# RWKV-7 inside a hybrid decoder layer: the substitution as a step of its own, the fourth unit prepared ahead of the third's solve

## The chip, the cores and the metric

One core of one Trainium2 chip. The metric is the device time of one execution in microseconds (us). A kernel's time is the median of several runs.

## What is computed

One layer of a decoder trunk on 1024 tokens of width 1024, in float32. One projection of the normalised input feeds three mixers side by side: a convolution group (256 columns), sparse attention (512 columns: 8 query heads with a compressed, a selected and a window branch) and RWKV-7 (256 columns: 4 heads of 64). Their outputs are put side by side, go through one output projection and are added to the residual; a gated feed-forward part follows. The change touches the RWKV part, which is, per head and token (cut from the reference, in its words shortened):

```
state = state * decay + (state @ -kk) outer (kk * a) + v outer k
y     = state @ r
y     = group_norm(y) * gain + bias
out   = (y + bonus * v) * gate
```

The recurrence is run in chunks of 32 tokens. Inside a chunk the terms that tie one token to the next form a triangular system; its inverse is built by substitution, row after row.

## The kernel before

Every product is float32 in three terms of high and low parts (`mm3`, L235, on TensorE; `split` makes the parts, L120 on ScalarE and L121 on VectorE). RWKV's work is cut into four units (j, h): j is a pair of heads, h a half of the tokens (512). Each unit passes three steps:

- start: `rwkv_prep` (decays, keys; L405 on) and `rwkv_mats` (L506 to L561). `rwkv_mats` makes the chunk matrices (L524 masks them, L538), stores the triangular ones to memory (`dn`, L529), makes `VA` and `KB` (L543, L544), loads all chunks' triangles into `sN` (L532) and runs the substitution on GpSimd, 31 pairs of a product and a sum (L554, L556), and stores the inverse (L560, L561).
- solve (`rwkv_solve`): loads the inverse into the tile that the triangles were in (`TT` is another view of `sN`) and applies it (L582, L589, L601 on TensorE).
- chain (`rwkv_chain`): the recurrence over 16 chunks (L617, L618, L623, L630, L634, L637), group norm (L643 to L654: mean, square on ScalarE, variance, an inverse root by Newton steps in `rsqrt`, L106 to L116), transposes (L657), gain and bias (`gz`, L659), bonus (L660), the gate product (L662, L663), and the store into `md` (L664).

`md` is a scratch tensor in memory that holds the three mixers' outputs. The steps are traced in the order of a string in L25; units (0, 0) and (0, 1) are traced ahead of attention's preparation, units (1, 0) and (1, 1) at the end of it. All steps of the units are traced with a high priority, and a scheduler then fixes every engine's order of instructions from its own model of when things are ready; on the chip each engine and SyncE's (SP) DMA queue keep that order.

Attention runs by query tiles in the order 7, 6, 5, 4, 0, 3, 2, 1 (`attn_tile`): compressed scores (L865 on TensorE, L870 and L873 on VectorE, L875 on GpSimd, L876 on ScalarE, L878 on VectorE, L883 on GpSimd, L888 and L891 on TensorE), then for four heads each a window and a selected branch (L919 and L920 scores, L923 mask and maximum from PSUM, L930 exponential, L932, L937 scaling of the probabilities, L944 transposes, L947, L952 product with the values). L958 takes a tile's result, L959 stores it to `md`. Beside it GpSimd makes sums of the feed-forward's down weights (`down_sums`, L971 to L974; loads L969, stores L977). They are tied to the substitutions: `issue_after(us[1, int(n > 1)].sub)`.

The output projection (`mix_load`, L1010; `out_tile`, L235, L1027) begins with tile 7 of the tokens, so with `md` columns that unit (1, 1) writes. Its weights are loaded at L994 and split in advance.

Of the kernel before, what the change touches and what calls it, by code (L numbers as in the profile page):

```python
# [19 lines left out]
class K:  # L20
    def __init__(self, tc, a, out, ctx, bufs=None):
        self.tc, self.nc, self.a, self.out, self.ctx = tc, tc.nc, a, out, ctx
        self.B = dict(b2=20, wraw=2, whi=2, wlo=2, t4=4, rraw=2, cy=2, hx=12, ev=3, cv=2, lora=2, rb=20, at=2, pr=7, rt=2,
                      QS=2, pp=6, q8=2, pT=5, pace=31, xn=8, ds=((), (0, 1, 2), (3, 4), (5, 6, 7), (8, 9), (10,), (), ()), h2=14, graw=2, prod=5, ft=4, u=4, wr2=4, wfh=3, wfl=3, S=2, p1=2, om=6, grow=2, pre=2, ap=(), wf=("own", "wf", "om"), hd=("vector",) * 4, tq=((0, 1, 2, 3),), ttag=("tr", "rw"),
                      mm=3, tr=2, av=1, rw=2, mm1=2, tr1=2, pm=2, early="00 01", ga=2, gb=1, gc=1, y=16, r4=15, ta=3, tb=4, mid=2, de=dict(S3="gpsimd", T3="vector", T1="gpsimd", T2="gpsimd", T4="vector", S1="gpsimd", S2="gpsimd", S4="gpsimd"), order=(7, 6, 5, 4, 0, 3, 2, 1), sc=0, pk=1280, st="sync", last=5, sub="gpsimd",  steps="lora r0 S00 conv taps pa V00 S01 pb keys q C00 V01 C01 r1a cmp0 cend r1b cmp1 r1c S10 V10 S11 C10 V11 C11", both=0, cm="gpsimd", rpu=(), wo="vector", tap=(0, 31), vt="cv", vs="vector", va={1: (0, 1), 3: (2, 3), 5: (4, 5), 7: (6, 7)}, vq="sync", vl=1, vw=1, t1=("pm", "tr1"), into={6: (6, 2), 4: (4, 2), 3: (3, 1), 2: (2, 1), 1: (1, 1), 0: (0, 1)})  # L25
        self.B.update(bufs or {})
        P_ = lambda n, **k: ctx.enter_context(tc.tile_pool(name=n, **k))
        self.cst = P_("cst", bufs=1)
        self.sm = P_("sm", bufs=4)
        self.big = P_("big", bufs=1)  # L30
        self.mcp = tc.tile_pool(name="mc", bufs=1)
        self.mc = self.mcp.__enter__()
        self.dram = P_("dram", bufs=1, space=bass.MemoryType.DRAM)
        self.uid = 0
        self.st = getattr(tc.nc, self.B["st"])
        self.xp = self.psp = None
# [470 lines left out]
    def rwkv_mats(self, u):  # L507
        nc = self.nc
        v, s, pe = nc.vector, nc.scalar, nc.tensor
        dn = self.dram.tile([32, 32, 32], F32, name=f"dn{u.j}{u.h}")  # L510
        u.dt = self.dram.tile([16, 32, 4, 8], F32, name=f"dt{u.j}{u.h}")
        u.dtt = self.dram.tile([32, 8, 4, 32], F32, name=f"dtt{u.j}{u.h}")

        u.GA, u.GR = ([self.rb([P, 8, 64], name=n) for _ in range(2)] for n in ("GA", "GR"))
        for q in range(2):
            pts = [self.bank(u.tp) for _ in range(2)]
            for c in range(4):
                for hp in range(2):
                    r = slice(hp * 64, hp * 64 + 64)
                    pe.matmul(pts[hp][:, c * P:c * P + P], u.BK[q][r, c].rearrange("p a t -> p (a t)"),  # L520
                              u.AR[q][r, c].rearrange("p a t -> p (a t)"), start=True, stop=True)
            for x, G in enumerate((u.GA, u.GR)):
                for hp in range(2):
                    v.tensor_tensor(G[hp][:, q * 4:q * 4 + 4, :], pts[hp].rearrange("p (a b) -> p a b", b=P)[:, :, x * 64:x * 64 + 64],  # L524
                                    self.gmask[:, x * 64:x * 64 + 64].unsqueeze(1).to_broadcast([P, 4, 64]), op=ALU.mult)
        for hp in range(2):
            for blk in range(2):
                p0 = blk * 16 + hp * 8
                nc.sync.dma_start(dn[p0:p0 + 8].rearrange("p s t -> s p t"), u.GA[hp][64 + blk * 32:96 + blk * 32, :, blk * 32:blk * 32 + 32])  # L529
        N = self.sN.rearrange("p (a b) -> p a b", b=32)  # L530
        for g in range(4):
            nc.sync.dma_start(N[g * 32:g * 32 + 32], dn)  # L532
        u.VA, u.KB = [], []
        for q in range(2):
            VA = self.rb([P, 4, P], name="VA")
            KB = self.rb([P, 4, P], name="KB")
            BK = u.BK[q].rearrange("p c a t -> p c (a t)")
            v.tensor_tensor(BK, BK, u.PC[:, q * 4:q * 4 + 4].unsqueeze(2).to_broadcast([P, 4, P]), op=ALU.mult)  # L538
            for dst in (VA, KB):
                pt = self.bank(u.tp)  # L540
                for c in range(4):
                    x = u.VAc[q][:, c].rearrange("p a t -> p (a t)") if dst is VA else BK[:, c, :]
                    pe.transpose(pt[:, c * P:c * P + P], x, self.idn)  # L543
                s.activation(dst.rearrange("p c x -> p (c x)"), pt, AF.Copy)  # L544
            u.VA.append(VA)
            u.KB.append(KB)

        Tm = self.sT
        nc.gpsimd.tensor_copy(Tm, self.sI)
        for q in range(31):  # L550
            n, w = 31 - q, q // 4 + 1
            x = self.sx[:, 0:n * w].rearrange("p (a b) -> p a b", b=w)
            v_ = getattr(nc, self.B["sub"])
            v_.tensor_tensor(x, N[:, q, q + 1:32].unsqueeze(2).to_broadcast([P, n, w]),  # L554
                            Tm[:, q, 0:w].unsqueeze(1).to_broadcast([P, n, w]), op=ALU.mult)
            u.sub = v_.tensor_tensor(Tm[:, q + 1:32, 0:w], Tm[:, q + 1:32, 0:w], x, op=ALU.add).ins  # L556
        sTT = self.sTT.rearrange("p a b -> p (a b)").rearrange("p (a b) -> p a b", b=32)
        v.tensor_copy(sTT, Tm.rearrange("p a b -> p b a"))
        for g in range(4):
            nc.sync.dma_start(u.dt[:, :, g, :], Tm[g * 32:g * 32 + 16])  # L560
            nc.sync.dma_start(u.dtt[:, :, g, :], sTT[g * 32:g * 32 + 32])  # L561
# [740 lines left out]
    def build(self):  # L1302
        order = self.B["order"]
        self.fill = []
        nc, a = self.nc, self.a
# [29 lines left out]
        us = {}  # L1335

        def start(j, h):
            with self.tc.high_priority(offset=100000):
                us[j, h] = self.rwkv_prep(j, h)
                self.rwkv_mats(us[j, h])  # L1340

        def solve(j, h):
            with self.tc.high_priority(offset=100000):
                self.rwkv_solve(us[j, h])

        def chain(j, h):
            with self.tc.high_priority(offset=100000):
                self.rwkv_chain(us[j, h])
        steps = dict(lora=lambda: self.rwkv_lora(hT), keys=lambda: self.attn_keys(hT), q=lambda: self.attn_q(hT),
                     cmp=lambda: self.attn_cmp(hT), conv=lambda: self.conv_proj(hT), taps=self.conv_taps, pa=lambda: self.conv_pool(range(20), us[0, 0].sub), pb=lambda: self.conv_pool(range(20, 31), us[0, 1].sub), cend=self.conv_rest, r0=lambda: self.rwkv_proj(0, hT),  # L1350
                     r1=lambda: self.rwkv_proj(1, hT), cmp0=lambda: self.attn_cmp(hT, (0,)), cmp1=lambda: self.attn_cmp(hT, (1,)),
                     r1a=lambda: self.rwkv_proj(1, hT, (0,)), r1b=lambda: self.rwkv_proj(1, hT, (1,)), r1c=lambda: self.rwkv_proj(1, hT, (2,)))
        for st in self.B["steps"].split():
            if st[0] in "SVC" and len(st) == 3:
                dict(S=start, V=solve, C=chain)[st[0]](int(st[1]), int(st[2]))
            else:
                steps[st]()
        self.phase("2")
# [86 lines left out]
```

## Time and profile before

| | us |
|---|---|
| median of 3 runs | 1489.62 (1488.12 to 1493.52) |
| the profiled execution | 1485.23 |
| its span, first to last instruction | 1483.7 |
| PE busy | 1396.1 (94%) |
| DVE busy | 1014.7 (68%) |
| ACT busy | 686.1 (46%) |
| POOL busy | 501.2 (34%) |

PE is TensorE's matmuls, PEld its weight loads, DVE VectorE, ACT ScalarE, POOL GpSimd, SP SyncE, whose instructions here are DMA issues. A matmul's end is modelled, so a busy PE is not PE at its peak. PEclk is TensorE's granted clock as a share of full speed. All times count from the span's start; attention lies between about 381 and 701 us. "idle before <-releaser" is the time in which the engine stood ahead of an instruction, and what ended it.

### The profile page before, as it was taken

What the parts mean: (1) busy time and instruction counts of PE and PEld (TensorE: products, weight loads), DVE (VectorE), ACT (ScalarE), POOL (GpSimd) and SP (SyncE); (2) the same over time, 40 slices, a digit from 0 to 9 for tenths busy, and PEclk for the clock granted to TensorE, in tenths of its full rate; (3) what the DMA queues carried; (4) which work ended last, traced back from release to release, by engine and by line L of the source; (5) the groups of instructions that cost most, each with busy time, mean ns of one, the idle gap of its engine ahead of it and who ended that gap; (6) DMA issues with size and microseconds to landing.
All of it is one profiled execution on the core that took longest, in us unless ns stands there. A gap on an engine that the chain in (4) does not pass through costs nothing.

```text
span 1483.7 us, 22736 instructions
## 1 busy us (share of the span) xinstructions
PE 1396.1 (94%) x7897; PEld 1100.5 (74%) x7897; DVE 1014.7 (68%) x2187; ACT 686.1 (46%) x1377; POOL 501.2 (34%) x607
## 2 busy tenths in 40 slices
PE   6999888899899999898799899999999999999997
PEld 5887666677677777576578677788788788888886
DVE  6343799355777788988357767676775776656685
ACT  5432454353466766677233443344333334445463
POOL 1001898830106407540000143443444452113310
PEclk9999898999899999999899899999999999999999
DMA  6133324525412612863641123332332334986523
GB/s 184 40 106 82 68 78 125 142 76 171 114 44 55 189 48 59 259 221 100 202 160 52 41 86 97 107 103 71 107 114 93 107 100 158 386 285 213 186 92 114
DMA packets 206678, 186.68 MB, mean 126 GB/s; under 512 B 56355, under 2 KB 145764, under 8 KB 206564
## 3 DMA queue, kind: packets, MB, share of 16 engines
q1 hardware_dynamic: 206564, 185.24, 40.2%
q8 instruction: 62, 1.02, 0.3%
q14 instruction: 52, 0.43, 0.1%
HBM read 126.99 MB, written 58.20 MB: 125 GB/s over the span
## 4 chain that ended last, share of the span: by engine, by line
PE 76%; DVE 11%; POOL 4%; issue 3%; DMA 3%; ACT 1%; SPq 1%; DVEq 0%; ACTq 0%; POOLq 0%
PE gb L235 13%; PE mm L235 10%; PE rw L235 10%; PE ga L235 9%; PE gc L235 8%; PE tr L235 5%; PE tr L944 4%; PE av L952 4%; PE mm L919 2%; POOL sT L556 2%; POOL sx L554 2%; PE mm L920 2%; DVE cacc L277 1%; DVE pp L923 1%; DVE pp L937 1%
## 5 line engine op out<-in xcount | busy, mean ns | idle before, releaser
L235 PE MATMUL mm<-hT,whi 128*128 128x512 f32 x608 | 198.4, 408 | 5.9 <-ACT whi L120 4.3
L235 PEld LDWEIGHTS mm<-hT,whi 128*128 128x128 f32 x608 | 116.2, 194 | 35.6 <-ACT whi L120 5.0
L235 PE MATMUL mm<-hT,wlo 128*128 128x512 f32 x304 | 123.6, 409 | 3.1 <-DVE wlo L121 2.9
L947 ACT ACTIVATE pT<-tr 128x512 f32<-128x512 f32 (+1 forms) x152 | 79.5, 534 | 46.6 <-PE tr L944 45.5
L294 POOL TENSOR_TENSOR cacc<-cacc,ctap 128x512 f32<-128x512 f32 x60 | 98.1, 1661 | 5.4 <-ACT ctap L292 4.7
L952 PE MATMUL av<-pT,V 128*64 128x128 f32 x1056 | 93.3, 287 | 1.6 <-ACT pT L947 1.6
L944 PE MATMUL tr<-idn,pp 128*128 128x128 f32 x528 | 90.7, 289 | 0.4 <-DVE pp L937 0.3
L121 DVE TENSOR_TENSOR sp<-rb,sp 128x512 fp32r<-128x512 f32 x66 | 56.6, 858 | 49.1 <-ACT sp L120 49.0
L235 PE MATMUL rw<-woh,mix 128*128 128x512 f32 x240 | 77.9, 400 | 9.5 <-ACT mix L120 6.6
L235 PE MATMUL rw<-sp,sp 128*128 128x512 f32 x330 | 86.2, 389 | 0.0
L235 PE MATMUL tr<-sp,sp 128*128 128x512 f32 x330 | 85.9, 389 | 0.0
L919 PE MATMUL mm<-KH,QS 128*128 128x512 f32 (+2 forms) x192 | 76.5, 403 | 9.2 <-DVE mx L923 8.0
L952 PEld LDWEIGHTS av<-pT,V 128*64 128x64 f32 x1056 | 56.9, 136 | 30.1 <-issue 15.8
L944 PEld LDWEIGHTS tr<-idn,pp 128*128 128x128 f32 x528 | 56.2, 141 | 30.3 <-issue 28.4
L120 ACT ACTIVATE sp<-rb 128x512 fp32r<-128x512 f32 x66 | 41.6, 630 | 74.4 <-PE tr L235 39.1
L121 DVE TENSOR_TENSOR sp<-b,sp 128x512 fp32r<-128x512 f32 x88 | 70.8, 814 | 4.9 <-ACT sp L120 4.8
L937 DVE TENSOR_SCALAR pp<-pp,sm 128x640 f32<-128x640 f32 (+7 forms) x128 | 72.9, 610 | 1.1
L235 PEld LDWEIGHTS mm<-hT,wlo 128*128 128x128 f32 x304 | 58.6, 193 | 18.5 <-DVE wlo L121 4.7
L1106 POOL TENSOR_TENSOR S<-wraw,wr 128x512 f32<-128x512 f32 x22 | 28.5, 1296 | 127.8 <-DVE wlo L121 46.7
L235 PEld LDWEIGHTS rw<-sp,sp 128*128 128x128 f32 x330 | 61.9, 188 | 13.1 <-ACT sp L120 0.3
L235 PEld LDWEIGHTS tr<-sp,sp 128*128 128x128 f32 x330 | 61.9, 188 | 12.9
L121 DVE TENSOR_TENSOR wlo<-wraw,whi 128x512 fp32r<-128x512 f32 x55 | 45.9, 837 | 35.2 <-ACT whi L120 32.9
(455 smaller groups left out, 3658.4 us busy)
## 6 DMA issues: line engine op xcount, KB each, us to landing
wraw<-in_ffn_w_up_dram SPq DMA_DIRECT2D x44, 256.0 KB
wr<-in_ffn_w_gate_dram SPq DMA_DIRECT2D x44, 256.0 KB
pdS<-prod SPq DMA_DIRECT2D x44, 256.0 KB
b<-pdS SPq DMA_DIRECT2D x44, 256.0 KB
rb<-tdT SPq DMA_DIRECT2D x44, 256.0 KB
pdA<-prod SPq DMA_DIRECT2D x33, 256.0 KB
b<-pdA SPq DMA_DIRECT2D x33, 256.0 KB
wraw<-in_w_in_dram SPq DMA_DIRECT2D x30, 256.0 KB
```

Of the source, the lines that this page charges most:

```text
L120: self.nc.scalar.activation(hi, src, AF.Copy)
L121: return getattr(self.nc, eng).tensor_tensor(lo, src, hi.bitcast(F32), op=ALU.subtract).ins
L235: mm = lambda l, r, **k: self.nc.tensor.matmul(out, l, r, skip_group_check=more, **k)
L294: nc.gpsimd.tensor_tensor(t[:, o:o + 512], t[:, o:o + 512], z, op=ALU.add)
L554: v_.tensor_tensor(x, N[:, q, q + 1:32].unsqueeze(2).to_broadcast([P, n, w]), Tm[:, q, 0:w].unsqueeze(1).to_broadcast([P, n, w]), op=ALU.mult)
L556: u.sub = v_.tensor_tensor(Tm[:, q + 1:32, 0:w], Tm[:, q + 1:32, 0:w], x, op=ALU.add).ins
L919: pe.matmul(pts[g][:, 0:n], QS[:, r, g, :], KH[g][hf][:, ks], start=True, stop=False)
L920: pe.matmul(pts[g][:, 0:n], QS[:, r, g, :], KL[g][hf][:, ks], start=False, stop=True)
L937: v.tensor_scalar(Ps[g], Ps[g], sm[:, g:g + 1], None, op0=ALU.mult)
L944: pe.transpose(pt[:, o:o + P], Ps[g][:, kt * P:kt * P + P], self.idn)
L947: s.activation(pT[:, 0:n], pt[:, 0:n], AF.Copy)
L952: pe.matmul(av[g * 64:g * 64 + 64, r * P:r * P + P], self.V[kk // 2][:, kk % 2, vo + g * 64:vo + g * 64 + 64], pT[:, o:o + P], start=first ...
```

## The change

`rwkv_mats` ends with `VA` and `KB`. What stood in it for the substitution, from the loads of `sN` to the stores of the inverse, becomes `rwkv_sub`, a step "B" of its own. In the string of steps B follows S at once for units (0, 0), (0, 1) and (1, 0); for unit (1, 1) the start now stands ahead of the solve of (1, 0), and the substitution behind that solve, whose tile it overwrites.

```
-steps="lora r0 S00 conv taps pa V00 S01 pb keys q C00 V01 C01 r1a cmp0 cend r1b cmp1 r1c S10 V10 S11 C10 V11 C11"
+steps="lora r0 S00 B00 conv taps pa V00 S01 B01 pb keys q C00 V01 C01 r1a cmp0 cend r1b cmp1 r1c S10 B10 S11 V10 B11 C10 V11 C11"
...
-        N = self.sN.rearrange("p (a b) -> p a b", b=32)
-        for g in range(4):
-            nc.sync.dma_start(N[g * 32:g * 32 + 32], dn)
+        u.dn = dn
         u.VA, u.KB = [], []
...
+    def rwkv_sub(self, u):
+
+        nc = self.nc
+        v, s = nc.vector, nc.scalar
+        N = self.sN.rearrange("p (a b) -> p a b", b=32)
+        for g in range(4):
+            nc.sync.dma_start(N[g * 32:g * 32 + 32], u.dn)
         Tm = self.sT
         nc.gpsimd.tensor_copy(Tm, self.sI)
...
+        def sub(j, h):
+            with self.tc.high_priority(offset=100000):
+                self.rwkv_sub(us[j, h])
+
...
-            if st[0] in "SVC" and len(st) == 3:
-                dict(S=start, V=solve, C=chain)[st[0]](int(st[1]), int(st[2]))
+            if st[0] in "SBVC" and len(st) == 3:
+                dict(S=start, B=sub, V=solve, C=chain)[st[0]](int(st[1]), int(st[2]))
```

The number of instructions on every engine stays. In the changed kernel most lines from the substitution on count five more (L561 is L556 of before, L662 is L657). The engines' orders are the same up to the second half of attention's tile 6 and from the first tiles of the output projection on; between them they differ, and the preparation of (1, 1) stands in tile 6 where it stood in tiles 5 and 4.

TensorE at the end of attention, before. `tr` and `av` are attention's transposes and value products of tile 1, `gyc` is the group norm's result of unit (1, 1), `mix` the mixers' output as loaded for the output projection:

```order
L952 MATMUL av_7701<-pT_7883,V_4513 64x128 x4
L944 MATMUL tr_7934<-idn,pp_7919 128x128 x4
L952 MATMUL av_7701<-pT_7911,V_4513 64x128 x4
L952 MATMUL av_7701<-pT_7939,V_4513 64x128 x4
L657 MATMUL rw_4413<-idn,gyc_4390 128x128 x4
L662 MATMUL rw_4421<-lora_772,lw_w 128x512
L235 MATMUL rw_8120<-woh_7950,mix_8040 128x512
```

And now:

```order
L957 MATMUL av_7701<-pT_7791,V_4513 64x128 x4
L662 MATMUL rw_4413<-idn,gyc_4390 128x128 x4
L667 MATMUL rw_4421<-lora_772,lw_w 128x512
L957 MATMUL av_7701<-pT_7819,V_4513 64x128 x4
L893 MATMUL tr_7825<-idn,cmp_7702 32x128 x4
L949 MATMUL tr_7850<-idn,pp_7835 128x128 x4
L896 MATMUL av_7701<-pT_7830,vcmp_4435 128x512
L949 MATMUL tr_7878<-idn,pp_7863 128x128 x4
L957 MATMUL av_7701<-pT_7855,V_4513 64x128 x4
L949 MATMUL tr_7906<-idn,pp_7891 128x128 x4
```

The unit's transposes and gate product stood between attention and the output projection; they stand among attention's last products now, eleven attention rows ahead of the first L235. On VectorE L665 and L668 (before L660 and L663) of that unit follow directly on the last L942 (before L937) of tile 1.

GpSimd at attention's tile 4, now. `cmp_6209` are that tile's compressed scores, L559 and L561 the substitution of unit (1, 1); before, both `cmp_6209` rows stood ahead of its first row:

```order
L559 TENSOR_TENSOR sx<-sN,sT 128x60
L561 TENSOR_TENSOR sT<-sT,sx 128x10x6
L880 TENSOR_TENSOR cmp_6209<-cmp_6209,cmx_6211 128x320
L559 TENSOR_TENSOR sx<-sN,sT 128x54
L561 TENSOR_TENSOR sT<-sT,sx 128x9x6
```

44 rows of the substitution stand ahead of this L880 and 15 more between it and the tile's L888. Of the sums of the down weights 18 now stand between the substitution and the first `cmp` row of tile 0, where 6 stood before, and 4 behind that of tile 3, where 16 stood.

TensorE in the solve of unit (1, 0), in attention's tile 5, now (`av_5665` is that tile's result, L896 its product with the compressed values, L891 before; L602 and L606 are the solve's, L597 and L601 before):

```order
L602 MATMUL rw_3981<-VA_3640,GA_3605 64x64 x4
L602 MATMUL rw_3981<-VA_3655,GA_3605 64x64 x4
L896 MATMUL av_5665<-pT_5906,vcmp_4435 128x512
L949 MATMUL tr_5948<-idn,pp_5911 128x128
L949 MATMUL tr_5948<-idn,pp_5912 128x128
```

Behind these rows come two more transposes, four value products, four transposes and then the solve's last eight L606, its last reading of `sN`; before, that last reading stood ahead of the tile's product with the compressed values. The loads of `sN` for unit (1, 1) wait for it.

## Rows read from the trace of the kernel before

**Rows 1.** Attention tiles 4, 1: PE, PEld, DVE, ACT, POOL busy, PEclk, DMA share

```profile
547.35:594.57 47.22, 46.95 (x433) 36.13 (x432) 40.19 (x162) 31.19 (x82) 27.51 (x70) 1.00 0.28 72
...
686.89:701.36 14.47, 13.00 (x129) 9.19 (x128) 11.62 (x46) 10.39 (x27) 0.80 (x2) 1.00 0.31 91
```

**Rows 2.** The same by equal stretches, two of them

```profile
600.00:640.00 40.00, 34.16 (x235) 21.08 (x234) 39.02 (x107) 24.93 (x61) 25.33 (x21) 0.91 0.77 253
...
710.00:720.00 10.00, 6.67 (x22) 5.37 (x23) 2.77 (x4) 2.52 (x4) 0.00 (x0) 0.65 0.64 168
```

**Rows 3.** PE's waits, 400 to 760 us: total, times, longest

```profile
PE rw L235 <- ACT mix L120: 6.6, 1, 6.6
PE mm L919 <- DVE mx L923: 6.0, 8, 2.4
```

**Rows 4.** PE's timeline at the end of attention: start, us, instruction

```profile
700.59 0.66 PE L952 MATMUL av<-pT,V 128*64 128x128 f32 x8 [0.18 <-ACT pT L947]
703.65 1.11 PE L657 MATMUL rw<-idn,gyc 128*128 128x128 f32 x4 [2.40 <-DVE gyc L654]
704.69 2.07 PE L662 MATMUL rw<-lora,lw_w 64*128 64x512 f32 x2
713.33 0.79 PE L235 MATMUL rw<-woh,mix 128*128 128x512 f32 x1 [6.56 <-ACT mix L120]
```

**Rows 5.** The chain of waits, 680 to 730 us: start, us, what

```profile
707.65 2.01 DMA md<-gz
709.74 2.88 DMA mix<-md
```

**Rows 6.** DVE's timeline, 693 to 718 us

```profile
694.05 0.61 DVE L937 TENSOR_SCALAR pp<-pp,sm 128x256 f32<-128x256 f32 x2
...
702.70 0.17 DVE L116 SCALAR_TENSOR_TENSOR gr<-rs_t,gr 128x8 f32<-128x8 f32 x1
...
705.61 0.69 DVE L660 TENSOR_TENSOR gz<-gz,bv 128x512 f32<-128x512 f32 x1 [2.02 <-ACT gz L659]
```

**Rows 7.** DVE's timeline at the start of tile 4

```profile
550.21 0.68 DVE L538 TENSOR_TENSOR BK<-BK,rPC 128x512 f32<-128x512 f32 x1
...
551.29 0.48 DVE L878 TENSOR_REDUCE csm<-cmp 128x8 f32<-128x320 f32 x1
```

**Rows 8.** POOL's timeline, 540 to 600 us

```profile
549.06 0.72 POOL L875 TENSOR_TENSOR cmp<-cmp,cmx 128x320 f32<-128x320 f32 x1 [42.55 <-ACT pT L947]
553.74 0.72 POOL L883 TENSOR_TENSOR cmp<-cmp,csm 128x320 f32<-128x320 f32 x1 [3.96 <-DVE csm L880]
557.63 0.24 POOL L554 TENSOR_TENSOR sx<-sN,sT 128x31 f32<-128x31 f32 x1 [3.17 <-DMA sN<-dn]
...
575.36 0.28 POOL L554 TENSOR_TENSOR sx<-sN,sT 128x54 f32<-128x54 f32 x1
...
580.69 0.22 POOL L556 TENSOR_TENSOR sT<-sT,sx 128x16 f32<-128x16 f32 x1
...
582.01 1.29 POOL L971 TENSOR_TENSOR wraw<-whi,wraw 128x512 f32<-128x512 f32 x1
```

**Rows 9.** DVE by line and form, 547 to 595, then 600 to 640 us

```profile
L937 DVE TENSOR_SCALAR pp<-pp,sm 128x640 f32<-128x640 f32 x14 | 7.5, 574 | 0.1
...
L937 DVE TENSOR_SCALAR pp<-pp,sm 128x512 f32<-128x512 f32 x16 | 13.6, 887 | 0.0
L923 DVE CUSTOM_DVE_ANT_0 pp<-mm,mwin 128x512 f32<-128x512 f32 x8 | 5.4, 677 | 0.8 <-PE tr L944 0.8
...
L660 DVE TENSOR_TENSOR gz<-gz,bv 128x512 f32<-128x512 f32 x1 | 1.8, 1753 | 0.0
```

**Rows 10.** PE's timeline in tile 5

```profile
523.05 1.02 PE L891 MATMUL av<-pT,vcmp 96*128 96x512 f32 x2
...
525.62 0.66 PE L952 MATMUL av<-pT,V 128*64 128x128 f32 x8
```

**Rows 11.** SP's timeline, 545 to 560 us

```profile
552.54 1.71 SPq L532 DMA_DIRECT2D sN<-dn  x4
```

More of the change, by code (lines that the diff above doesn't have):

```diff
@@ L24, in __init__ @@
                       QS=2, pp=6, q8=2, pT=5, pace=31, xn=8, ds=((), (0, 1, 2), (3, 4), (5, 6, 7), (8, 9), (10,), (), ()), h2=14, graw=2, prod=5, ft=4, u=4, wr2=4, wfh=3, wfl=3, S=2, p1=2, om=6, grow=2, pre=2, ap=(), wf=("own", "wf", "om"), hd=("vector",) * 4, tq=((0, 1, 2, 3),), ttag=("tr", "rw"),
-                      mm=3, tr=2, av=1, rw=2, mm1=2, tr1=2, pm=2, early="00 01", ga=2, gb=1, gc=1, y=16, r4=15, ta=3, tb=4, mid=2, de=dict(S3="gpsimd", T3="vector", T1="gpsimd", T2="gpsimd", T4="vector", S1="gpsimd", S2="gpsimd", S4="gpsimd"), order=(7, 6, 5, 4, 0, 3, 2, 1), sc=0, pk=1280, st="sync", last=5, sub="gpsimd",  steps="lora r0 S00 conv taps pa V00 S01 pb keys q C00 V01 C01 r1a cmp0 cend r1b cmp1 r1c S10 V10 S11 C10 V11 C11", both=0, cm="gpsimd", rpu=(), wo="vector", tap=(0, 31), vt="cv", vs="vector", va={1: (0, 1), 3: (2, 3), 5: (4, 5), 7: (6, 7)}, vq="sync", vl=1, vw=1, t1=("pm", "tr1"), into={6: (6, 2), 4: (4, 2), 3: (3, 1), 2: (2, 1), 1: (1, 1), 0: (0, 1)})
+                      mm=3, tr=2, av=1, rw=2, mm1=2, tr1=2, pm=2, early="00 01", ga=2, gb=1, gc=1, y=16, r4=15, ta=3, tb=4, mid=2, de=dict(S3="gpsimd", T3="vector", T1="gpsimd", T2="gpsimd", T4="vector", S1="gpsimd", S2="gpsimd", S4="gpsimd"), order=(7, 6, 5, 4, 0, 3, 2, 1), sc=0, pk=1280, st="sync", last=5, sub="gpsimd",  steps="lora r0 S00 B00 conv taps pa V00 S01 B01 pb keys q C00 V01 C01 r1a cmp0 cend r1b cmp1 r1c S10 B10 S11 V10 B11 C10 V11 C11", both=0, cm="gpsimd", rpu=(), wo="vector", tap=(0, 31), vt="cv", vs="vector", va={1: (0, 1), 3: (2, 3), 5: (4, 5), 7: (6, 7)}, vq="sync", vl=1, vw=1, t1=("pm", "tr1"), into={6: (6, 2), 4: (4, 2), 3: (3, 1), 2: (2, 1), 1: (1, 1), 0: (0, 1)})
         self.B.update(bufs or {})
```

## The prediction, written before the change was run

> **What bounds the kernel now.** The profiled execution took 1485.23 us (span 1483.7); the median of the runs shown is 1489.62, 4.39 us above it. The sum below is made against the profiled execution and then moved up by that. About 7.4 us (0.5% of 1489.62) is what a measurement of this kernel can tell from no change.
>
> I read the table by attention tiles first [rows 1]. TensorE (PE) is busy 46.95 of 47.22 us in tile 4 at clock 1.00, so attention as a whole is PE's. The table by equal stretches [rows 2] shows two other places: 600 to 640, where PE falls to 34.16 of 40 us, the clock to 0.91, and VectorE (DVE) is busy 39.02; and 710 to 720, where PE is busy 6.67 of 10 at a clock of 0.65. The list of PE's waits names them [rows 3]: the output projection waits 6.6 us for ACT's split of the mixers' output (L120), and attention's scores (L919) wait 6.0 us in eight pieces for DVE's masking.
>
> PE's timeline shows the hole at the end of attention [rows 4]: the last value product starts at 700.59 and ends at 701.25; then 2.40 us idle, the transposes and gate product of RWKV's last unit (1.11 and 2.07), 6.56 us idle, and the first product of the output projection at 713.33. From 701.25 to 713.33 are **12.08 us**, 3.2 of them work. The chain of waits says what fills the rest [rows 5]: gz's store to memory (2.01) and the load back (2.88), behind group norm and gate and ahead of the split. All of it is the tail of unit (1,1): the recurrence ends after attention does.
>
> **Boundary.** The change adds and removes no instruction; it moves them. Unit (1,1)'s transposes and gate product now stand among the last attention products, with eleven attention rows of PE between them and the output projection, and its gz operations on DVE stand directly behind the last probability scaling (L937). Those L937 end at 694.66 [rows 6]. Behind them gz needs two operations of 0.69 (L660, L663): 696.0. In the trace the store was issued at 707.65, as soon as L663 ended, and the first product came 5.68 later [rows 4, 5]: 701.7. The attention itself would end at 701.25 plus the moved PE work, 3.2 us at half clock, so 1.6 at full: 702.9. The mixers' output would be there 1.2 us before PE is. I still leave 1.0 us of hole (0 by these rows; 7.7, from L660's start at 705.61 to 713.33, if gz slips behind the last tile again). Gain: 12.08 - 1.6 - 1.0 = **9.5**, bounds 2.8 to 10.5.
>
> **Clock behind it.** A mean of 0.65 over 710 to 720 is 7.0 us at the lower level, 1.2 GHz [rows 2], after PE stood nearly idle since 701. Of these 3.3 are the hole, so 3.7 us of products ran at half speed. Without the hole 1.8 us come back at most, and none if what follows waits for loads (DMA is 0.64 busy there). I take **1.0**.
>
> **Attention, DVE.** Here lies the price. Tile 4 has DVE busy 40.19 of 47.22, so 7.0 idle [rows 1]. Unit (1,0)'s chain and group norm come earlier; the norm and gz, some 6.5 us of DVE (six operations like 705.61's 0.69 and fourteen like 702.70's 0.17 [rows 6]), move from tiles 0 and 3 into tile 4. In return the last preparation of (1,1), still at 550.21 in that tile [rows 7], goes to tile 6, and part of (1,0)'s chain to tile 5. Tiles 0 and 3 lose the norm and get the solve and a part of (1,1)'s chain. (1,1)'s own norm now falls ahead of the last L937, 6.5 us near tile 1, where DVE idles 2.9 of 14.5 [rows 1], but the chain that stood there has gone up. Bounds: 6.5 lost if none of the norm finds a hole, 5.8 won if PE's idle time in 600 to 640 (40 - 34.16 [rows 2]) goes. I take **1.0 lost**: what comes to a tile left its neighbour, and both had idle time.
>
> GpSimd's (POOL) sums of the down weights move too: 12 more of them come ahead of tile 0's scores and leave the stretch behind tile 3's. Where POOL was busy 25.33 us with sums of 1.29, some 18 of them [rows 2, 8], L937 on 128x512 took 887 ns; 640 wide in tile 4 it took 574, so 512 wide should be near 490: 16 x 0.4 = 6.4 us; L660 took 1753 ns against 0.69 [rows 6, 9]. These alone are 7.5 us, 0.4 per sum; with the small operations beside them I put it at **0.6 us of DVE per sum**, an estimate, so 12 are 7 us that leave tile 3 and enter tile 4. L923, which reads PSUM, took 677 ns beside the sums [rows 9], the 0.69 of an untouched pass of that size. I count the move as nothing on balance; rival B prices it. The Trainium skill ("SBUF — State Buffer", section "Who interferes with whom") says that DVE and GpSimd share one port pair as an exclusive lock, which speaks against putting sums beside tile 4's scalings; the trace agrees in kind. By that rule alone tile 4 would grow by what tile 3 gives back, and the sum stay as it is.
>
> **Substitution on POOL.** The new order puts tile 4's L875 behind 44 of the substitution's instructions and L883 behind 59; both stood ahead of it. In the trace the substitution starts at 557.63 and its 45th instruction at 575.36: 17.7 us [rows 8]. L875 ran at 549.06, so N would have to land by 531.3. Its load waits for the third solve's last product, which the order puts behind tile 5's product with the compressed values, 523.05 in the trace, and three groups of transposes and values: a start near 525.6 and, as the row there of 0.66, an end at 526.3 [rows 10]. In the trace the first N load was issued at 552.54 and the substitution began 5.1 us later [rows 8, 11]: 526.3 + 5.1 = 531.4. That just fits: DVE's L878 ran at 551.29 [rows 7], 1.5 us behind L875's end, ACT's exponential between them, so about 1.0 us are slack. I take **0.5 lost**, bounds 0 and 18 (rival D). The substitution itself, ending 27 us earlier, is off PE's path and is what lets the rest move up. On SP's queue gz's store now stands ahead of tile 1's result instead of behind it.
>
> **Sum.** 9.5 + 1.0 - 1.0 - 0.5 = 9.0 gained: 1485.23 - 9.0 = 1476.2, on the median's scale 1489.62 - 9.0 = **1480.6**. With what the terms may be off together this case reaches from 1477 to 1484.
>
> **Rivals.**
> *B, attention gives it back.* Tile 4 becomes DVE's: 6.5 of norm and 7 of stretch come, with 7.0 idle there, and in 600 to 640 DVE could leave only 1 us of 40 unused. What is over by some 6.5 is lost, and tile 3 finds no use for what it gets back: 9.0 + 1.0 - 6.5 = 3.5 gained, 1486. For it: 39.02 of 40 shows how far it goes. Against: preparation and part of the chain leave that tile.
> *C, tiles 0 and 3 ease too.* Twelve sums and a norm leave the only stretch where DVE holds PE. PE's 5.8 us there go: 14.8 gained, 1475. For it: the waits for L923 [rows 3]. Against: the solve and chain of (1,1) come in.
> *D, slower.* POOL is in order, and so is DVE behind L878. If the N load lands only as tile 4 begins, about 547.35 (behind a weight load on SP that waits for its buffer, or a solve that PE reaches late), L875 follows 17.7 us later at 565.0 and L883, behind 59 instructions (580.69 less 557.63, 23.1) and L875's 0.7, at 571.1 instead of 553.74, 17.4 us late [rows 8]. DVE, and then PE, stand for all but the 1.0 of slack, and a clock that falls in such a hole costs 1.8 more (above): 9.0 - 18.2 = -9.2, 1499. The point: each microsecond past 532.4 costs one, 9 eat the gain, 16 make it slower by over 0.5%. For it: the margin is 1.0 us by my estimate. Against: the load's place is 21 us ahead of 547.35.
> *E, the hole stays.* The chain's steps wait for each other as before, PE, in order, idles inside the last tile instead of behind it, and gz comes no earlier: 1489.
>
> **How the numbers follow.** Forecast 0.45, B 0.18, C 0.14, D 0.12, E 0.11. Faster by over 0.5% (under 1482.2): C, 0.8 of the forecast, and a little of B: 0.14 + 0.36 + 0.02 = 0.52. Slower (over 1497.0): 0.07 of D and 0.02 of the far ends of B and E, 0.09. Same: the rest, 0.39. The range takes the forecast, B, E, and most of C, and leaves most of D and C's far end out: 1472 to 1492.
>
> **What would show it.** Right: at the end of attention no PE wait over 2 us, clock 1.00 across it, the first product of the output projection within 3 us of the last value product, gz's store issued ahead of tile 1's; the substitution of (1,1) begins near 531 on POOL; tile 4 has DVE busy above 43 us. C: PE's waits in tiles 0 and 3 are gone. Wrong: a DVE wait of several microseconds at tile 4's L878 (D); tile 4 longer than 50 us with DVE nearly full (B); the same hole, or one inside tile 1 (E).

## The result, and the profile after

| | before | changed |
|---|---|---|
| median of 4 runs (us) | 1490.53 (1488.12 to 1493.52) | 1476.99 (1475.74 to 1479.58) |
| ratio | | 0.991, 95% interval 0.9887 to 0.9934 |
| profiled execution | 1485.23 | 1477.66 |
| its span | 1483.7 | 1475.8 |

The change makes the kernel 13.5 us faster. That is more than the 9.0 forecast. By the number alone it lies at the lower edge of the forecast case (1477 to 1484) and 2 us from case C's 1475; the rows decide between the two, and they show the forecast case: the hole at the end of attention is gone.

TensorE's timeline of the changed kernel, at the end of attention (start, us, instruction; lines count five more than before):

```profile
699.52 0.65 PE L662 MATMUL rw<-idn,gyc 128*128 128x128 f32 x4
700.10 1.12 PE L667 MATMUL rw<-lora,lw_w 64*128 64x512 f32 x2
701.15 0.66 PE L957 MATMUL av<-pT,V 128*64 128x128 f32 x8
...
707.84 0.66 PE L957 MATMUL av<-pT,V 128*64 128x128 f32 x8 [0.16 <-ACT pT L952]
708.42 0.50 PE L235 MATMUL rw<-woh,mix 128*128 128x512 f32 x1
708.76 0.39 PE L235 MATMUL rw<-wol,mix 128*128 128x512 f32 x1
```

Against [rows 4], the transposes and the gate product of unit (1,1) run eight microseconds before attention ends, at full speed (0.65 where 1.11 stood, 1.12 where 2.07), and the output projection follows the last value product without a gap. SP's queue shows why:

```profile
695.67 0.38 SPq L964 DMA_DIRECT2D md<-mix  x1
702.54 0.33 SPq L669 DMA_DIRECT2D md<-gz  x1
704.62 4.79 SPq L1015 DMA_DIRECT2D mix<-md  x3
709.60 0.36 SPq L964 DMA_DIRECT2D md<-mix  x1
```

gz's store goes at 702.54, before tile 1's result (709.60), and the load follows 2.1 us later, as in [rows 5]. TensorE's waits from 400 to 760 us no longer have the line of 6.6 us [rows 3], and those for the masking fell from 6.0 to 2.8:

```profile
PE av L957 <- ACT pT L952: 3.1, 3, 2.4
PE mm L924 <- DVE mx L928: 2.8, 5, 0.9
PE rw L235 <- DVE xn L1032: 2.4, 2, 1.5
PE rw L662 <- DVE gyc L659: 2.3, 1, 2.3
```

The two equal stretches that answer to [rows 2] (PE, PEld, DVE, ACT, POOL busy, PEclk, DMA share, GB/s):

```profile
600.00:640.00 40.00, 36.33 (x368) 25.60 (x366) 33.63 (x119) 25.42 (x74) 22.84 (x20) 1.00 0.83 267
...
710.00:720.00 10.00, 9.60 (x43) 7.62 (x41) 1.86 (x3) 1.90 (x3) 0.00 (x0) 1.00 0.97 276
```

DVE has room in 600 to 640 now, and the clock is 1.00 in both. But other work stands in that stretch: before, tiles 0 and 3; now, the end of tile 4 and tile 0. So the tiles themselves have to be compared (from one tile's result, L958 or L963, to the next, and how long TensorE is idle in it, us):

| tile | before | changed | difference | TensorE idle before | TensorE idle changed |
|---|---|---|---|---|---|
| 6 | 51.2 | 59.1 | +7.9 | 1.2 | 3.4 |
| 5 | 50.4 | 55.1 | +4.7 | 0.3 | 0.2 |
| 4 | 48.2 | 49.9 | +1.7 | 0.3 | 4.5 |
| 0 | 19.8 | 24.9 | +5.1 | 2.5 | 0.2 |
| 3 | 45.2 | 32.4 | -12.8 | 3.3 | 0.0 |
| 2 | 26.7 | 23.8 | -2.9 | 0.3 | 0.0 |
| 1 | 15.1 | 13.9 | -1.2 | 1.5 | 0.6 |
| all seven | 256.6 | 259.1 | +2.5 | 9.3 | 8.9 |

Tiles 0 and 3 before, then tiles 4, 0 and 3 of the changed kernel (columns as above):

```profile
594.59:614.37 19.78, 17.26 (x105) 10.55 (x104) 18.52 (x62) 12.19 (x37) 12.18 (x12) 0.91 0.92 296
614.37:659.56 45.19, 41.87 (x424) 30.39 (x423) 38.97 (x105) 29.62 (x71) 25.56 (x21) 0.96 0.74 240
```

```profile
563.90:613.80 49.90, 45.42 (x378) 32.06 (x376) 46.78 (x164) 29.34 (x79) 29.66 (x38) 1.00 0.62 183
613.80:638.70 24.90, 24.68 (x276) 17.99 (x274) 19.26 (x65) 17.02 (x47) 14.70 (x13) 1.00 0.84 275
638.70:671.10 32.40, 32.40 (x293) 23.05 (x292) 30.22 (x101) 25.64 (x63) 6.56 (x6) 1.00 0.50 155
```

Attention is not shorter: preparation went from tiles 5 and 4 to 6, solve and chains from tiles 3, 2 and 1 to earlier ones, and the sum grew by 2.5 us, 1.6 of which is the moved tail of unit (1,1). TensorE's idle time moved with the work: 5.6 us of it left tiles 0 and 3, and 6.4 came to tiles 6 and 4, where VectorE is now busy for 50.4 of 59.1 and 46.8 of 49.9 us.

### The profile page after: what moved, and what is told of

It reads as the page before. It is cut to its first block, busy times and chain, and to the rows that moved or that the text cites. A ratio compares the mean times of both kernels' runs of the same rounds, so it can differ in the third digit from the quotient of the medians.

```text
span 1475.8 us, 22749 instructions
## 1 busy us (share of the span) xinstructions
PE 1395.3 (95%) x7897; PEld 1099.7 (75%) x7897; DVE 1006.8 (68%) x2187; ACT 684.7 (46%) x1377; POOL 504.1 (34%) x607
## 4 chain that ended last, share of the span: by engine, by line
PE 73%; DVE 10%; POOL 7%; DMA 4%; issue 3%; ACT 2%; SPq 1%; DVEq 0%; POOLq 0%; ACTq 0%
PE gb L235 13%; PE mm L235 11%; PE ga L235 9%; PE rw L235 9%; PE gc L235 9%; PE tr L235 5%; PE av L957 4%; PE tr L949 3%; POOL sT L561 3%; POOL sx L559 2%; POOL cacc L294 2%; PE mm L924 2%; DMA mix<-md 2%; PE mm L925 1%; DVE pp L942 1%
## 5 line engine op out<-in xcount | busy, mean ns | idle before, releaser
L235 PE MATMUL mm<-hT,whi 128*128 128x512 f32 x608 | 201.0, 413 | 7.7 <-ACT whi L120 7.1
L235 PEld LDWEIGHTS mm<-hT,whi 128*128 128x128 f32 x608 | 118.1, 197 | 38.3 <-ACT whi L120 8.6
L235 PE MATMUL mm<-hT,wlo 128*128 128x512 f32 x304 | 125.5, 415 | 4.5 <-DVE wlo L121 4.3
L235 PE MATMUL rw<-sp,sp 128*128 128x512 f32 x330 | 86.0, 389 | 0.0
L235 PE MATMUL tr<-sp,sp 128*128 128x512 f32 x330 | 85.9, 389 | 0.0
L235 PE MATMUL rw<-woh,mix 128*128 128x512 f32 x240 | 76.7, 395 | 2.4 <-DVE xn L1032 2.4
L120 ACT ACTIVATE sp<-rb 128x512 fp32r<-128x512 f32 x66 | 41.6, 630 | 74.2 <-PE tr L235 37.5
L235 PEld LDWEIGHTS mm<-hT,wlo 128*128 128x128 f32 x304 | 59.6, 196 | 19.8 <-DVE wlo L121 5.6
L121 DVE TENSOR_TENSOR wlo<-wraw,whi 128x512 fp32r<-128x512 f32 x55 | 47.8, 871 | 37.7 <-ACT whi L120 35.5
L559 POOL TENSOR_TENSOR sx<-sN,sT 128x60 f32<-128x60 f32 (+24 forms) x124 | 43.2, 348 | 88.2 <-DMA sN<-dn 79.2
L235 PEld LDWEIGHTS rw<-sp,sp 128*128 128x128 f32 x330 | 62.0, 188 | 12.9
L235 PEld LDWEIGHTS tr<-sp,sp 128*128 128x128 f32 x330 | 61.9, 188 | 12.9
```

What stands on the lines that cost most here:

```text
L120: self.nc.scalar.activation(hi, src, AF.Copy)
L121: return getattr(self.nc, eng).tensor_tensor(lo, src, hi.bitcast(F32), op=ALU.subtract).ins
L235: mm = lambda l, r, **k: self.nc.tensor.matmul(out, l, r, skip_group_check=more, **k)
```

## The experiments

All ratios are to the kernel before, run on the same chip in the same session.

**The wait taken out of the kernel before.** Unit (1,1)'s gz isn't stored, so nothing of the recurrence stands between attention and the output projection's load:

```
-        self.st.dma_start(self.md[:, 2 + j, u.h * 512:u.h * 512 + 512], z)
+        if (j, u.h) != (1, 1):
+            self.st.dma_start(self.md[:, 2 + j, u.h * 512:u.h * 512 + 512], z)
+        if (j, u.h) == (0, 1):
+            self.st.dma_start(self.md[:, 3, 512:1024], z)
```

> The kernel before, but the output projection does not wait for unit (1,1): that unit's gz is not stored, and unit (0,1) stores its own into both pairs of columns, so that part of the output is another unit's. Orders of all engines stay apart from the missing store and a few rows behind the boundary. Theory (the hole at the end of attention is what the change removes, and it is worth its length): the first product of the output projection comes behind L662 at about 706.8 instead of 713.3 on the trace's clock, since the load can go as soon as tile 1's result is stored; PE's 2.4 us wait for L654 stays. 6.5 us and about 1 for the clock: ratio to the kernel before 0.995, some 7 us faster. Rival 1 (what follows is bound by loads, the hole is filled later): within 2 us of before. Rival 2 (the gain of the change comes from inside attention): also within 2 us.

Measured: 1488.58 (median of 10) against 1492.74 us, ratio 0.998 (0.996 to 0.9999). The hole is 7.8 us instead of 12.1, so 4.3 us shorter, and the kernel 3.0 us faster by the ratio, with an interval from 0.1 to 6.0. That interval alone doesn't exclude the rivals' 2 us; the profile speaks against both. From the projection's first product to the end it is 770.3 us, 770.4 in the kernel before, so the loads didn't fill the hole again (rival 1), and from tile 7's result to the last value product it is 256.9, 256.5 before, so nothing inside attention gave the time (rival 2). But 6.5 us were expected. TensorE's timeline and SP's queue of this run:

```profile
710.07 1.12 PE L662 MATMUL rw<-lora,lw_w 64*128 64x512 f32 x2
714.91 0.79 PE L235 MATMUL rw<-woh,mix 128*128 128x512 f32 x1 [3.72 <-ACT mix L120]
```

```profile
707.82 0.38 SPq L962 DMA_DIRECT2D md<-mix  x1
711.27 5.69 SPq L1013 DMA_DIRECT2D mix<-md  x4
```

The queue is free from 708.2 and the load goes at 711.27, just when L662 has ended. There is a second lock.

**The second lock.** The load's tile comes from a pool opened where the pool of the RWKV operands is closed. The same cut, with the gate product L662 issued ahead of the group norm:

```
+        if (j, u.h) == (1, 1):
+            pg = self.bank("rw")
+            pe.matmul(pg, self.lw_w[64:128, j * P:j * P + P], self.L[u.h][64:128], start=True, stop=True)
         m = self.small([P, 8], "gm1")
...
         v.tensor_tensor(z, z, u.bv, op=ALU.add)
-        pg = self.bank("rw")
-        pe.matmul(pg, self.lw_w[64:128, j * P:j * P + P], self.L[u.h][64:128], start=True, stop=True)
+        if (j, u.h) != (1, 1):
...
```

> The kernel before with the same cut as in the first experiment (unit (1,1)'s gz is not stored, unit (0,1) stores into both pairs of columns, so that part of the output is another unit's), and unit (1,1)'s gate product L662 moved ahead of its group norm, eleven rows earlier on TensorE. In the first experiment the load of the mixers' output was issued only when L662 had ended, 3.1 us after the queue was free; its tile may take over the memory of L662's operands, whose pool is closed at that point. Theory (that memory is the second lock): the load goes within 1 us of tile 1's store, the hole between the last value product and the output projection is 4.5 to 6 us instead of 7.8, 2 to 3 us faster than that experiment. Rival (the lock is another tile of the unit's tail, gyc or gz): the hole stays at 7 us or more.

Measured: 1486.89 against 1490.87 us, ratio 0.9973 (0.9951 to 0.9996), the hole 6.9 us. The chain of waits, and SP's queue:

```profile
711.77 0.67 PE rw L660 x4
712.47 0.79 ACT gz L662
713.27 0.36 SPq L1017
713.68 3.83 DMA mix<-md
```

```profile
710.81 0.38 SPq L966 DMA_DIRECT2D md<-mix  x1
```

The load now goes when the gz activation ends (713.27), 2.1 us after the queue is free instead of 3.1. So L662's operands were a lock, and behind them the operands of the next instruction of the tail are another; with a hole of 6.9 us the rival was the nearer one. What the two runs show is that the load waits for the tail's instructions without any data from them. The addresses in the built kernels say why. The load's tile takes bytes 120160 to 122208 of each partition, where `lw_w` lay (121408 to 122432), which L662 reads, and `par` (120960 to 121316), the gain and bias that the gz activation reads. The two tiles that the rival named are not the lock: `gyc` and `gz` lie elsewhere, and in the first cut VectorE still wrote `gz` at 712.32, behind the load. In time the second cut can't be told from the first: 4.0 us (0.6 to 7.3) below the kernel before, where 2 to 3 more than the first cut's 3.0 were expected. In the changed kernel all these instructions end by 702.5, so one move opened all the locks.

**The same cut in the changed kernel.**

> The changed kernel with the same cut: unit (1,1)'s gz is not stored, unit (0,1) stores into both pairs of columns, so that part of the output is another unit's. Theory (the tail is hidden completely in the changed kernel): nothing left to gain, within 2 us of 1477. Rival (the tail still delays the loads or the projection): 3 us or more faster than the changed kernel.

Measured: 1486.02 (1481.56 to 1492.20), ratio 0.9953 (0.9935 to 0.9971): neither, it is slower than the changed kernel. The hole is 0.3 us, so at the boundary nothing is left to gain, but the cut changed two things beside it. The scheduler put the residual's load behind loads of feed-forward weights on SP, 727.57 instead of 712.29, and TensorE waits 5.5 us for L1035 (2.4 for L1032 in the changed kernel). And in the profiled execution, the slowest of the six, the clock fell to its lower level inside attention and stayed there (two stretches of the table, behind one in which TensorE was busy 7.83 of 10 us):

```profile
611.00:621.00 10.00, 10.00 (x94) 7.55 (x92) 5.99 (x25) 4.64 (x16) 4.34 (x5) 0.50 0.62 200
621.00:631.00 10.00, 10.00 (x75) 7.86 (x75) 6.71 (x14) 3.17 (x7) 5.18 (x5) 0.50 0.91 283
```

Tile 0 took 34.3 us there. As a measure of the tail in the changed kernel this run is inconclusive; its hole is the part that counts.

**The changed kernel again**, because of that result.

> The changed kernel unchanged, beside the others, because the cut with the store left out came out 6 us slower than the changed kernel had been. Theory (the clock's spells at the lower level fall differently from execution to execution and make the scatter): median again about 0.991 of the kernel before, single executions within some 10 us of each other, and the profiled execution's low-clock time explains where it lies in that range. Rival (the first measurement of the changed kernel was a lucky one): 0.995 or above.

Measured: 1477.57 (1474.56 to 1490.77), ratio 0.9908 (0.9875 to 0.9941). The gain stands, and one execution in six was 13 us above the median. It is the one with the lowest mean granted clock, 0.961, against 0.970 to 0.975 in the others, as the theory of the scatter has it.

**Early preparation without the early tail.** The solve of (1,1) is traced ahead of the chain of (1,0):

```
-S10 B10 S11 V10 B11 C10 V11 C11
+S10 B10 S11 V10 B11 V11 C10 C11
```

> The changed kernel with the solve of (1,1) traced ahead of the chain of (1,0): preparation and substitution of (1,1) stay as early as in the change, but both chains move back, and the transposes and gate product of (1,1) stand again directly ahead of the output projection's first product. Theory (the hole is the gain): a hole of 8 to 12 us is back between the last value product and the output projection, 8 to 13 us slower than the changed kernel, 1485 to 1490. Rival (the gain comes from taking the preparation and the substitution out of tiles 5 and 4): stays within 3 us of 1477.

Measured: 1498.59 (1492.08 to 1509.70), ratio 1.0041 (1.0016 to 1.0066), some 20 us slower than the changed kernel and slower than the kernel before. Preparation and substitution are as early as in the change; attention's seven tiles are even shorter, 253.8 us, in part because the last of the chain's products fall behind them; but the chains end late, and the hole, with those products in it, is 21.6 us. TensorE's waits:

```profile
PE rw L662 <- DVE gyc L659: 8.9, 1, 8.9
PE rw L235 <- ACT mix L120: 6.5, 1, 6.5
```

The theory had the sign, and the hole came out twice as long as expected. The rival, that the gain lies in taking the preparation out of tiles 5 and 4, is out.

**The split alone** (the new step traced at once behind the start, in the old order of units) gives every engine the same instructions in the same order as the kernel before, so it wasn't run. The changed order with B11 behind C10 gives the order of the changed kernel. What the change does is the place of one step: S11 ahead of V10. A substitution ahead of that solve would need a second tile for the triangles, 4 KB in each partition, which doesn't fit beside the other pools; that wasn't tried on the chip.

**Sums out of tiles 4 and 0.**

```
-ds=((), (0, 1, 2), (3, 4), (5, 6, 7), (8, 9), (10,), (), ())
+ds=((), (0, 1, 2), (3, 4), (), (), (5, 6), (7, 8), (9, 10))
-                with self.tc.issue_after(us[1, int(n > 1)].sub):
+                with self.tc.issue_after(self.cm_ins if n > 4 else us[1, int(n > 1)].sub):
```

> The changed kernel with the down-weight sums of tiles 4 and 0 traced behind tiles 3, 2 and 1, tied to those tiles' compressed scores. Theory (place of the sums is neutral, what tile 4 gains a later tile loses): within 3 us of 1477. Rival B (sums stretch DVE in tiles 4 and 0, which are tight, and tiles 2 and 1 have room): tiles 4 and 0 together 4 to 7 us shorter, tiles 2 and 1 hardly longer, 1471 to 1474. Third case: the sums collide with the loads of the output projection's weights and its splits, slower than 1480.

Measured: 1510.49, ratio 1.0123 (1.0103 to 1.0143), the third case. Tiles 4 and 0 did lose 7.1 us (45.9 and 21.8), tiles 3, 2 and 1 grew by 8.2, and a hole of 12.4 us opened at the boundary, with another 21 us lost behind it. The hole isn't the tail's this time: TensorE waits for the split of the projection's weights (`woh`, L120), whose loads now stand on SP's queue among the loads and stores of the sums. From this run's page:

```profile
L235 PE MATMUL rw<-woh,mix 128*128 128x512 f32 x240 | 82.7, 418 | 29.4 <-ACT woh L120 29.0
```

**Sums out of tile 6**, twelve of them, and sixteen:

```
-ds=((), (0, 1, 2), (3, 4), (5, 6, 7), (8, 9), (10,), (), ())
+ds=((), (), (0, 1, 2), (3, 4, 5, 6, 7), (8, 9), (10,), (), ())
-                with self.tc.issue_after(us[1, int(n > 1)].sub):
+                with self.tc.issue_after(self.cm_ins if n == 2 else us[1, 1].sub):
```

> The changed kernel with the first twelve down-weight sums taken out of tile 6, where the preparation of (1,1) now stands, and put on GpSimd in tile 5, between that tile's compressed scores and the substitution; all else stays near its place. In the changed kernel VectorE is busy 50 of 59 us in tile 6 and 36 of 55 in tile 5. Theory (each sum costs VectorE some 0.6 us beside it, and tile 6 is the one place where that is on TensorE's path): VectorE's busy time falls by 5 to 7 us in tile 6, TensorE's idle 3.3 us there and the low-clock spell behind it go, tile 6 is 3 to 5 us shorter, tile 5 at most 1 longer; 3 to 5 us faster than the changed kernel, ratio to the kernel before 0.988 or below. Rival (the stall in tile 6 is the burst of preparation itself, as the copy's move to ScalarE suggests): tile 6 within 1 us, total within 2 us of the changed kernel. Other way out: the sums' loads and stores push the load of the triangles back, the substitution starts later and tile 4 waits for it, 2 us or more slower.

> The same with four more sums in tile 5 (sixteen, some 22 us of GpSimd ahead of the substitution, in a gap of 28 us). Theory: as above, and tiles 0 and 3, which get four sums less, up to 2 us shorter. Rival (the sixteen and their DMA reach into the substitution): its start later than the 36 us that it has behind the start of tile 5 in the changed kernel, tile 4 longer by the same.

Measured: 0.991 (0.9883 to 0.9938) for twelve and 0.9926 (0.9901 to 0.9951) for sixteen; not faster than the changed kernel. With twelve, tile 6 took 54.1 us, 5.0 less than in the changed kernel, as the theory had it, and tile 5 took 59.7, 4.6 more, which it had not. With sixteen they took 54.1 and 57.7; the substitution starts 39.3 us into tile 5 there, behind the rival's 36, and tile 4 is 2.1 us longer, though L880 waits 2.2 us for VectorE and not for the substitution. The small operations of VectorE in tile 6 show the relief (by line and form, first two rows of the changed kernel, then of the run with twelve):

```profile
L933 DVE TENSOR_TENSOR nm<-mx 128x2 f32<-128x2 f32 x8 | 2.9, 364 | 0.1
L937 DVE TENSOR_TENSOR sm<-sm,gates 128x2 f32<-128x2 f32 x7 | 2.3, 335 | 0.1
```

```profile
L933 DVE TENSOR_TENSOR nm<-mx 128x2 f32<-128x2 f32 x8 | 1.9, 236 | 0.1
L937 DVE TENSOR_TENSOR sm<-sm,gates 128x2 f32<-128x2 f32 x8 | 1.4, 180 | 0.1
```

Over the whole tile VectorE's busy time fell from 50.4 to 44.5 us with twelve, and in tile 5 it rose from 36.0 to 42.1: 0.5 us per sum in either place. TensorE's idle time went from 3.4 to 0.9 us in tile 6 and from 0.2 to 3.3 in tile 5. From tile 7's result to the output projection's first product it is 258.2 and 257.6 us in these two, 258.5 in the changed kernel, 259.6 when that was run again. Where the sums stand decides which tile is long, not how long attention is, as long as they stay clear of the loads of the projection's weights.

**The copy of the inverse off VectorE**, first to ScalarE, then to GpSimd. In the changed kernel a new stall stands in tile 6: VectorE waits 2.8 us for the substitution of (1,0) ahead of this copy, and TensorE's timeline shows what follows:

```profile
490.43 0.39 PE L924 MATMUL mm<-KH,QS 128*128 128x256 f32 x1 [0.82 <-DVE mx L928]
...
493.37 1.12 PE L957 MATMUL av<-pT,V 128*64 128x128 f32 x8 [2.44 <-ACT pT L952]
```

```
-        v.tensor_copy(sTT, Tm.rearrange("p a b -> p b a"))
+        s.activation(sTT, Tm.rearrange("p a b -> p b a"), AF.Copy)
```

> The changed kernel with the transposed copy of the inverse (L563) on ScalarE instead of VectorE, in all four units. In the changed kernel's trace VectorE stands 2.8 us in tile 6 for the substitution's last step ahead of this copy, the preparation of (1,1) comes in a burst behind it, and TensorE idles 3.3 us and then runs some 4 us at a clock of 0.65. Theory (this new wait costs 4 to 5 us): 3 to 5 us faster than the changed kernel, tile 6 from 59 to about 55 us. Rival (VectorE is the bound in tile 6 anyway, 50.4 of 59 us, so only the copy's own 1.5 us go, or ScalarE now waits in its place): within 2 us.

> The changed kernel with the transposed copy of the inverse on GpSimd, behind the substitution that it copies. Theory of the wait in tile 6: 3 to 5 us faster than the changed kernel, less what the solve starts later (two sums of 1.3 us now stand ahead of the copy), so 0 to 4 us faster. Rival (GpSimd's queue makes the solve late and the tail of (1,1) slips back to the boundary): slower than the changed kernel by 2 us or more.

Measured: 0.9899 (0.9876 to 0.9923) with ScalarE, 0.9919 (0.9893 to 0.9945) with GpSimd, both the same as the changed kernel's 0.9908 within the intervals. VectorE's wait for the substitution is gone from the list in both, and tile 6 is still 59.6 and 61.4 us. The rival holds: in its place VectorE waits 2.1 us for TensorE's L468, and with the copy on ScalarE it is busy 51.7 of 59.6 us, where it was 50.4 of 59.1. The run with twelve sums fewer in this tile says the same from the other side: its wait ahead of the copy is still 2.8 us, and the tile is 5.0 us shorter. VectorE's work there limits, not the wait. No version of this section was measurably faster than the changed kernel.

**TensorE kept busy in the hole** of the kernel before, five products that nobody reads behind L662:

```
+        if (j, u.h) == (1, 1):
+            with self.tc.issue_after(g_.ins):
+                pd = self.bank("rw")
+                for i in range(5):
+                    pe.matmul(pd, self.lw_w[64:128, 0:P], self.L[u.h][64:128], start=True, stop=True)
```

> The kernel before with five idle products on TensorE behind the gate product at the end of attention, about 5 us of work at full speed, whose result nobody reads. Theory (the products behind the hole run at half speed because TensorE stood idle, which is worth 1.8 us): the products of the output projection run at clock 1.00 from the first, which comes no later than 713.3 on the trace's clock; 1 to 2 us faster than before, within its scatter. Rival (the low level has another cause, or the loads bound what follows): the first products again 0.43 apart, or the gain is lost by the third tile.

Measured: 1496.25 against 1491.94 us, ratio 1.0034 (1.0012 to 1.0056), slower. The products took 8 us, and the load, which the second lock keeps until the last reader of those operands, went only behind them, at 724.30. gz's store had gone at 718.11, so for its data the load could have gone at 720.2, by the 2.1 us of [rows 5]:

```profile
716.11 8.12 PE L667 MATMUL rw<-lora,lw_w 64*128 64x512 f32 x10
727.94 0.80 PE L235 MATMUL rw<-woh,mix 128*128 128x512 f32 x1 [3.70 <-ACT mix L120]
```

So it doesn't answer its question, what the clock behind the hole costs; it shows the lock once more, and that the projection's first products run at half speed behind 3.7 us of idleness too.

## Why the prediction held, step by step

The sum's terms, measured between tile 7's result (444.75 before, 449.93 after) and the end:

| term | forecast | measured |
|---|---|---|
| boundary: 12.08 less moved work less hole | +9.5 (1.6 moved, 1.0 hole) | +10.4 (1.6 moved, no hole) |
| clock behind it | +1.0 | +1.7 after 12 us, +2.1 after 50 |
| attention, DVE | -1.0 | -0.4 with the next |
| substitution on POOL | -0.5 | |
| behind attention, not forecast | | +0.9 |
| sum | +9.0 | +13.1 |

- **The mechanism was right, the size was short by 4 us**, three rows of the sum a little on the careful side and 0.9 us that nobody forecast. First product to first product it is 268.6 and 258.5 us, 10.1 gained (10.4 less 0.4, rounded). From there to the end 770.4 and 767.4. Of these 3.0, 1.7 stand in the first 12 us, as the half-speed products of [rows 4] would have it. That they last isn't shown: with V11 ahead of C10 the projection's first 4 us ran at a clock of 0.50, behind a hole of 21.6 us, and the stretch from the first product to the end took 766.2 us all the same, 1.2 less than in the changed kernel. The last 0.9 is chance; it came at 813 to 836 us, where the clock stood at its lower level for 10.2 us in the execution before and 6.8 in the one after, in work that the change doesn't touch. In the changed kernel's second profile it was 10.2 us there again.
- **The hole is the cause by other kernels too.** Against the kernel before, holes shorter by 4.3 and 5.2 us (the two cuts; in the second the gate product, 1.1 us, moved into attention instead) go with 3.0 and 4.0 us less time, a hole longer by 3.7 (the idle products) with 5.1 more. With V11 ahead of C10 the first product came 6.8 us later behind tile 7's result, and the kernel was 6.1 us slower. These four agree to 1.4 us. The change's 10.1 and 13.4 differ by 3.3, and 3.0 of it are the stretch behind the first product.
- **The profiled executions differ by only 7.9 us in span** although the sum is 13.1, because 5.2 were lost ahead of the change. The same products, in the same order, ran at a clock of 1.00 in one execution and 0.52 in the other (first row before, second row after):

```profile
330.00:340.00 10.00, 10.00 (x109) 7.78 (x108) 4.20 (x16) 3.58 (x8) 0.00 (x0) 1.00 0.09 28
```

```profile
330.00:340.00 10.00, 10.00 (x53) 7.80 (x53) 2.87 (x17) 2.11 (x5) 0.00 (x0) 0.52 0.01 2
```

  The profiled execution of before, 1485.23, is below all four runs of its median. The difference of the medians, 13.5, agrees with the 13.1.
- **Gz directly behind the last scaling.** Right. The load took the time of [rows 5]. The split (L120, from 707.68) ended at 708.30, 0.1 us ahead of the first product, where the text had 1.2 in hand. The 1.0 left for a hole was not needed, but by little.
- **Attention: moved work is conserved.** Right, and better supported than its argument was: over the changed kernel, its second run and four relatives with other places of sums or copies, a tile differs by up to 7.3 us (tile 6, 54.1 to 61.4) and the whole, to the first product, by 2.2 (257.6 to 259.8). The three other variants have a hole or a long low-clock spell in that stretch and are left out.
- **B and C both came true by half**, and the halves cancel. B had tile 4 become DVE's: it did, with DVE busy 46.8 of 49.9 us and TensorE idle for 4.5 of them instead of 0.3, 2.3 in one wait for unit (1,0)'s group norm; the sign set for B, longer than 50 us, was missed by 0.1 (in the second run it was 50.8). C had TensorE's idle time in tiles 0 and 3 go: it did, from 5.8 to 0.2 us. What refutes B is that tile 3 used what it got back, and what refutes C is that tiles 6 and 4 took it. The forecast had the balance, not the places. (C's sum leaves in the 1.0 lost that B's takes out; without it C is 15.8 gained and 1474.)
- **0.6 us of DVE per sum** was an estimate a little too high: twelve sums fewer in tile 6 took 5.9 us of VectorE's busy time away, 0.49 each, between the two figures of the text, and twelve more in tile 5 brought 6.2. The Trainium skill ("SBUF — State Buffer", section "Who interferes with whom") has VectorE and GpSimd share a pair of ports as an exclusive lock. The trace agrees in kind: L933 took 364 ns with the sums beside it and 236 with twelve fewer. That attention's total doesn't pay is what the runs add.
- **Substitution on POOL, rival D.** The absolute time, 531, was wrong: it started at 545.47, 14 us later, as tile 7's end was 5.2 us later, tile 6 7.9 longer and tile 5 4.7. But L880, which it had to make way for, also came 15.1 us later than L875 before, so it fitted. Some of that was luck: the solve's last product ended 33.5 us into tile 5, not 30.4, and from the load to the first instruction it was 2.9 us, not 5.1.

```profile
562.12 0.31 POOL L561 TENSOR_TENSOR sT<-sT,sx 128x60 f32<-128x60 f32 x1
564.16 0.72 POOL L880 TENSOR_TENSOR cmp<-cmp,cmx 128x320 f32<-128x320 f32 x1 [1.74 <-DVE cmx L878]
...
570.87 0.97 POOL L888 TENSOR_TENSOR cmp<-cmp,csm 128x320 f32<-128x320 f32 x1 [0.81 <-DVE nm L933]
```

  The 44 instructions end at 562.43 and L880 waits 1.74 us for VectorE, not for the substitution (a margin of 1.0 was forecast); L888 too. D didn't happen, with a margin small enough to keep it a fair rival. (The text's "27 us earlier" for the end of the substitution is 25.5 by its own rows; nothing hangs on it.)
- **What the prediction missed**: the stall in tile 6 (TensorE idle for 0.82 and 2.44 us in the rows above, its value products behind that at 1.12 us instead of 0.66). The text let the preparation go to tile 6 at no cost. DVE went from 37.7 busy in 51.2 us to 50.4 in 59.1, and TensorE idled 2.2 us more there. The runs tie it to VectorE's work in that tile and not to the copy's wait. It didn't change the sum, since tile 3 gave as much back.

## What to carry to other kernels

Where a long recurrence runs beside a stage that keeps TensorE busy, look for its tail at the stage's end, and read the gap there from three queues at once (TensorE, the DMA queue, the chain of waits): a gap that has one cause in the list of waits may have several locks. Here no cut of one lock took more than 5.2 of the 12.1 us, and ending the whole tail earlier opened them all. What this reorder did inside the full stage cancelled to 0.4 us; its worth was read from the gap, and a step's place in the trace order counts only if an engine's order changes with it.

## What the runs showed that was not expected

- A load whose data were there still waited for the last readers of the tiles of a closed pool whose memory its own tile takes: in turn L662 (711.27), the filler products (724.30) and the gz activation (713.27).
- TensorE's clock differs between executions of the same code in the same order: at 329 us it stood at 1.2 GHz for 10.2 us in the profiled changed kernel and not at all in the profiled kernel before, 4.3 us of time, and for 3.4 us in the changed kernel's second profile. Behind a 2.2 us gap near 610 us it stayed there for 27 us in one run and for no time in another. Such spells are as large as what is measured here, so a single execution says little about a change of 10 us: the changed kernel's ten runs span 1474.56 to 1490.77.
- Tracing one step earlier by one place (V11 ahead of C10) costs 20 us, more than the change gains.
